# Spreads by transposes, a softmax without its sign flip, a new order of attention's weight loads, and eight fixed PSUM banks from the last head pair on

## The chip, the cores and the metric

The kernel runs on one core of one Trainium2 chip. The metric is the device time of one execution, in microseconds (us). A core has a matrix engine (TensorE, PE), a vector engine (VectorE, DVE), a scalar engine (ScalarE, ACT), GpSimd (POOL) and a queue that issues most DMAs (SyncE, SP). Each engine works through its own list of instructions in order and waits on semaphores for the others. TensorE writes to PSUM, eight banks of 512 float32 per partition.

## The reference, cut to what matters

One block of a network over 512 latent tokens of width 2048 and 256 context tokens, in float32:

```
mod = silu(c) @ w_ada + b_ada                       # six vectors of 2048, for shift, scale and gate
h   = modulate(rms_norm(x, g_mix), shift_a, scale_a)
qa, kva, kr, cb, cc, ch = split(h @ w_in)           # the context goes through the same weights
k, v = mla_key_value(kva, kr, g_kv, w_kv, rope)     # latent and context keys and values, 8 heads
q    = mla_query(qa, g_q, w_q, rope)                # rms_norm(qa, g_q) @ w_q
p    = softmax(q @ k.T * 192 ** -0.5)               # 512 queries, 768 keys
att  = p @ v
conv = cb * dwconv3(cc * ch)
x    = x + gate_a * (rms_norm per group of 128 of [att, conv]) @ w_out
hf   = modulate(rms_norm(x, g_ffn), shift_f, scale_f)
x    = x + gate_f * (a * silu(g)) @ w_down          # a, g = split(dwconv3(hf @ w_up))
out  = rms_norm(x, g_final)
```

## The kernel before, in words

Activations lie transposed, channels on partitions and tokens on columns. A product in float32 precision is made of three passes: each operand is split into a rounded high part (a CAST on ACT, names ending in `h`) and the rest (a subtraction on DVE, names ending in `l`), and TensorE adds high by high, low by high and high by low (`mm3`, L170 to L172). So every weight tile that arrives by DMA in a raw buffer costs an ACT and a DVE instruction before its matmuls.

The stages, in order of time: loads, norm and the first modulation vectors (to about 100 us); the input projection and the context (to 436); attention (to 652); the output projection, six of whose 16 output groups run as **rows** (`row`: one of 16 blocks of the input against six output groups, 18 matmuls, tiles `of`, to 714) and the other ten as **wholes** (`whole`, tiles `o6` to `o13`, then `o14` and `o15` by halves in the tile `ol`, to 831); the first three column groups of the up projection as rows again (tiles `uf`, to about 900); the other up products `u3`, `u4`, ... by a scheme of seven products for eight (tiles `u3a`, `u3b`, `u3c`; `u3p6`, `u3q5` are its weights), to 1683; the down projection to the end.

**Attention** is a loop of 32 steps, (head, quarter of the queries), in four pairs of heads. A step makes the scores two steps ahead (`scores`, tile `s`), takes a row maximum on DVE (L683), multiplies it by minus the scale (L684), does Exp on ACT with row sums (L687, tile `p`), transposes `p` on TensorE (L700, tile `t`), splits it (`pth`, `ptl`), and every second step multiplies with the values (`attend`, tile `po`). Spread through the loop are: the pieces of the next pair's queries, keys and values (`pieces`, weights `rq`, `rk`, loaded by `fetch`), the dots of the later modulation vectors (`late_dot`, L238: 1 MB `ra` loads by `late_load`, two DVE instructions of 1024 columns each), and the norms of finished heads: `merge_sum` makes the sums of a pair (tile `gs`), GpSimd takes a power (L732, tile `gr`), and `merge` spreads the result (tile `gb`). `late_bg` holds the same for the convolution's groups, four of them before the loop's steps and four behind them (`gn`, `acc21` to `acc30`). The `ra` loads and the weights of queries, keys and values share the two raw buffers of the pool `wp`.

A **spread** turns a column of 128 numbers into a 128 by 128 tile whose every row is that column: a matmul of the broadcast column with the identity (`spread`, L267, and the same in `merge`, L741).

A tile scheduler orders each engine's list from the program's order and its own estimates of durations; `keep` holds some instructions (the dots among them) in the program's order. PSUM is two pools' worth of rotating tiles: two tiles of two banks (`big`: `s`, `rs`, `ol`, parts of the rows) and four of one bank (`sml`: `t`, `po`, `gs`, `gb`, `pq`). When the up products from `u3` on begin, these pools are closed and eight fixed banks take their place (`bank_of`, `BANKS`).

When the rows of the up projection are through, `acts` does the width-3 convolution and the silu (L928 to L938, with one load of the Silu table) of their three column groups; its place is inside `u3`, between the products `p2` and `p6`.

## Time and profile before

| | |
|---|---|
| median of 3 runs | 2206.74 us (2206.45 to 2209.09) |
| the profiled execution | 2206.8 us, of which the span 2204.9 and 1.9 around it |
| PE busy in the span | 2149.2 us (97%) |
| DVE, ACT, POOL busy | 1599.0, 1010.5, 111.3 us |
| mean granted clock of TensorE | 0.996 |

Rows of the profile give a start or a stretch, the busy time, engine, line, operation and the tiles written and read; a bracket gives the idle time ahead of an instruction and the engine whose result ended it. A busy PE is a modelled figure: matmuls overlap, and a row that gives 0.28 us for one of 256 columns stands among rows that start every 0.12 us. The granted clock (PEclk) is 1.00 at full speed.

### The profile page before, as it was taken

What the parts mean: (1) busy time and instruction counts of PE and PEld (TensorE: products, weight loads), DVE (VectorE), ACT (ScalarE), POOL (GpSimd) and SP (SyncE); (2) the same over time, 40 slices, a digit from 0 to 9 for tenths busy, and PEclk for the clock granted to TensorE, in tenths of its full rate; (3) what the DMA queues carried; (4) which work ended last, traced back from release to release, by engine and by line L of the source; (5) the groups of instructions that cost most, each with busy time, mean ns of one, the idle gap of its engine ahead of it and who ended that gap; (6) DMA issues with size and microseconds to landing.
All of it is one profiled execution on the core that took longest, in us unless ns stands there. A gap on an engine that the chain in (4) does not pass through costs nothing.

```text
span 2204.9 us, 34542 instructions
## 1 busy us (share of the span) xinstructions
PE 2149.2 (97%) x13346; PEld 1914.2 (87%) x13346; DVE 1599.0 (73%) x2493; ACT 1010.5 (46%) x1635; POOL 111.3 (5%) x149
## 2 busy tenths in 40 slices
PE   7899999999999999999999999999999999999998
PEld 4688888878888888899999999999999888888887
DVE  7998887678896848777777777777777873633544
ACT  5523333544452237555554555555554432532444
POOL 0000000000000000011111011111110000000000
PEclk9999999999999999999999999999999999999999
DMA  8989884434469925577777777777776995753462
GB/s 331 344 276 334 275 279 150 144 120 149 158 235 358 331 86 172 132 196 201 204 194 195 201 205 195 194 201 201 201 193 200 350 345 159 247 164 92 160 210 88
DMA packets 144264, 466.75 MB, mean 212 GB/s; under 512 B 16290, under 2 KB 20642, under 8 KB 138082
## 3 DMA queue, kind: packets, MB, share of 16 engines
q1 hardware_dynamic: 125652, 405.03, 54.1%
q0 software_dynamic: 16272, 57.42, 12.8%
q8 instruction: 104, 1.70, 0.3%
q10 hardware_dynamic: 2176, 2.10, 0.3%
q14 instruction: 60, 0.49, 0.1%
HBM read 442.73 MB, written 20.71 MB: 210 GB/s over the span
## 4 chain that ended last, share of the span: by engine, by line
PE 91%; DVE 4%; DMA 2%; ACT 2%; issue 1%; SPq 0%; POOL 0%; DVEq 0%; ACTq 0%
PE d L170 7%; PE d L172 7%; PE d L171 7%; PE pp L170 4%; PE pp L172 4%; PE pp L171 4%; PE o L172 1%; PE o L171 1%; PE o L170 1%; PE uf L170 1%; PE uf L171 1%; PE uf L172 1%; PE of L172 1%; PE pf L171 1%; PE of L170 1%; PE of L171 1%
## 5 line engine op out<-in xcount | busy, mean ns | idle before, releaser
L997 POOL DMA_DIRECT2D u_s<-in_w_up x80 | 68.1, 851 | 416.3 <-DMA u_s<-in_w_up 353.4
L153 ACT CAST w_0h<-rw 128x512 fp32r<-128x512 f32 (+1 forms) x63 | 38.5, 618 | 107.3 <-PE pp L171 65.7
L216 DVE SCALAR_TENSOR_TENSOR ada<-ada,sv 128x1024 f32<-128x1024 f32 x64 | 77.4, 1217 | 4.6 <-DMA ada<-in_w_ada 4.6
L491 DVE SCALAR_TENSOR_TENSOR ada<-ada,svc 128x1024 f32<-128x1024 f32 x64 | 75.9, 1218 | 2.0 <-DMA ada<-in_w_ada 1.8
L238 DVE SCALAR_TENSOR_TENSOR ra<-ra,sv 128x1024 f32<-128x1024 f32 x50 | 59.4, 1216 | 0.0
L154 DVE TENSOR_TENSOR w_0l<-rw,w_0h 128x512 fp32r<-128x512 f32 (+1 forms) x63 | 42.4, 680 | 21.8 <-ACT w_0h L153 21.8
L238 DVE SCALAR_TENSOR_TENSOR ada<-ada,sv 128x1024 f32<-128x1024 f32 x46 | 55.7, 1218 | 2.6 <-DMA ada<-in_w_ada 2.6
L1108 DVE TENSOR_TENSOR u<-u,u 128x1024 f32<-128x1024 f32 x40 | 49.0, 1225 | 1.3
L1107 DVE TENSOR_TENSOR u<-u,u_s 128x1024 f32<-128x1024 f32 x40 | 48.7, 1217 | 0.0
L939 POOL DMA_DIRECT2D y_d<-a x43 | 24.7, 576 | 386.2 <-DVE a L938 376.7
L732 POOL TENSOR_TENSOR gr<-gr,half 128x8 f32<-128x8 f32 x4 | 8.3, 2084 | 641.4 <-DVE mx L684 505.3
L238 DVE SCALAR_TENSOR_TENSOR adl<-adl,sv 128x1024 f32<-128x1024 f32 x32 | 38.8, 1218 | 0.2 <-DMA adl<-in_w_ada 0.2
L683 DVE TENSOR_REDUCE mx<-s 128x1 f32<-128x768 f32 x32 | 30.4, 951 | 8.4 <-PE s L673 8.4
L704 DVE TENSOR_TENSOR ptl<-t,pth 128x384 fp32r<-128x384 f32 x64 | 33.2, 548 | 4.2 <-ACT pth L703 4.2
L502 DVE TENSOR_TENSOR acc<-acc,pp 128x512 f32<-128x512 f32 x50 | 33.9, 678 | 1.9 <-PE pp L172 1.8
L703 ACT CAST pth<-t 128x384 fp32r<-128x384 f32 x64 | 28.5, 488 | 14.3 <-PE t L700 14.1
L936 ACT ACTIVATE g<-g 128x512 f32<-128x512 f32 x43 | 27.2, 633 | 12.1 <-DVE g L930 12.1
L928 ACT ACTIVATE g<-cg,sm 128x512 f32<-128x512 f32 x40 | 32.5, 813 | 0.0
L687 ACT ACTIVATE p<-s,mx 128x768 f32<-128x768 f32 x32 | 29.3, 915 | 6.8 <-DVE mx L684 6.6
L928 ACT ACTIVATE a<-ca,sm 128x512 f32<-128x512 f32 x40 | 32.1, 802 | 0.0
L700 PE MATMUL t<-io,p 128*128 128x128 f32 x192 | 27.5, 274 | 3.7 <-ACT p L687 2.4
L929 DVE SCALAR_TENSOR_TENSOR g<-cg,sm,g 128x511 f32<-128x511 f32 x40 | 29.8, 745 | 0.0
(15580 smaller groups left out, 8734.8 us busy)
## 6 DMA issues: line engine op xcount, KB each, us to landing
ada<-in_w_ada SPq DMA_DIRECT2D x174, 512.0 KB, 6.0
u<-in_w_up SPq DMA_DIRECT2D x120, 512.0 KB, 8.3
u_s<-in_w_up SPq DMA_DIRECT2D x80, 512.0 KB, 4.1
u_s<-in_w_up POOLq DMA_DIRECT2D x80, 512.0 KB, 9.5
d<-in_w_dn SPq DMA_DIRECT2D x86, 384.0 KB, 3.8
y<-y_d SPq DMA_DIRECT2D x129, 256.0 KB, 4.5
ra<-in_w_ada SPq DMA_DIRECT2D x25, 1024.0 KB, 4.8
adl<-in_w_ada SPq DMA_DIRECT2D x32, 512.0 KB, 6.0
```

The lines of the kernel that those rows point to most:

```text
L153: A.copy(out=hi[:, :n], in_=raw[:, a:a + n])
L154: V.tensor_tensor(out=lo[:, :n], in0=raw[:, a:a + n], in1=hi[:, :n].bitcast(F32), op=ALU.subtract)
L170: PE.matmul(ps, w[0], x[0], start=first, stop=False, skip_group_check=on_top)
L171: PE.matmul(ps, w[0], x[1], start=False, stop=False, skip_group_check=on_top)
L172: PE.matmul(ps, w[1], x[0], start=False, stop=last, skip_group_check=on_top)
L216: V.scalar_tensor_tensor(out=r, in0=r, scalar=1.0, in1=vec[:, i * 1024:(i + 1) * 1024], op0=ALU.mult, op1=ALU.mult, accum_out=col[:, i:i + 1])
L238: keep(V.scalar_tensor_tensor(out=r, in0=r, scalar=1.0, in1=svs[i], op0=ALU.mult, op1=ALU.mult, accum_out=lc[:, t % 4:t % 4 + 1] if i else ...
L491: keep(V.scalar_tensor_tensor(out=raw[q], in0=raw[q], scalar=1.0, in1=svc[:, q * 1024:(q + 1) * 1024], op0=ALU.mult, op1=ALU.mult, accum_o ...
L928: A.activation(u, src, AF.Identity, bias=s("fb", m), scale=s("fw", 86 + m))
L997: G_.dma_start(r[-1], src[more], accum_op=ALU.add)
L1107: V.tensor_tensor(out=a11, in0=a11, in1=s1, op=ALU.add)
L1108: V.tensor_tensor(out=a12, in0=a12, in1=a11, op=ALU.add)
```

## The change

It has these parts:

1. The gain of the queries `g_q` is multiplied by minus the scale once at the start, so scores come out negative and scaled: a step takes the row minimum and Exp with scale -1, and the small multiplication L684 is gone (32 instructions).
2. `spread` is a transpose of the broadcast column against the identity, in place of a matmul, and `merge` uses it: 88 spreads in the whole kernel.
3. A dummy Exp stands behind the last square root ahead of attention, so that the Exp table is loaded there.
4. The loads of attention's weights are issued one to three steps ahead at the start of each pair, and the next pair's first piece `q_nope(1, 0)` stands ahead of the loop; the `ra` loads stand in six steps of eight, up to step 28 (22 of them, before 25); `merge` comes one step later, the last four convolution groups come in the steps 25, 27, 29 and 31, and the first two weights of the output projection's rows are loaded in the steps 29 and 30.
5. PSUM becomes eight fixed banks when the loop's steps end. The last `attend`, the last `merge_sum` and then four of the 16 rows (`OUT_EARLY`) come ahead of the last `merge`. `ol`, `uf` and the norm behind them get fixed banks, and the order of `BANKS` differs.
6. Of the three `acts` that stood inside `u3`, one stays there, one comes at the end of `u3`'s step and one at the end of `u4`'s.

```diff
-            PE.matmul(pb[:, g * P:(g + 1) * P], bc(r[:, g:g + 1], P), ident, start=True, stop=True)
+            PE.transpose(pb[:, g * P:(g + 1) * P], bc(r[:, g:g + 1], P), ident)
...
+        V.tensor_scalar(s("g_q", 0, 4), s("g_q", 0, 4), scalar1=-SCALE, scalar2=None, op0=ALU.mult)
...
-            mx = tiny(1, f"mx{hd}{tt}")
-            V.tensor_reduce(mx, ss[:, :768], axis=AX.X, op=ALU.max)
-            V.tensor_scalar(mx, mx, scalar1=-SCALE, scalar2=None, op0=ALU.mult)
+            mn = tiny(1, f"mn{hd}{tt}")
+            V.tensor_reduce(mn, ss[:, :768], axis=AX.X, op=ALU.min)
...
-            A.activation(pt, ss[:, :768], AF.Exp, bias=mx, scale=SCALE, accum_out=den[hd // 2][:, i:i + 1])
+            A.activation(pt, ss[:, :768], AF.Exp, bias=mn, scale=-1.0, accum_out=den[hd // 2][:, i:i + 1])
...
+        with tc.issue_after(roots[0]), tc.issue_after(roots[1]):
+            A.activation(tiny(1, "exp"), eps, AF.Exp)
+        fetch(1, 0)
+        late_load(ada_raw)
...
+        q_nope(1, 0)
+        fetch(1, 1)
...
-            elif n % 8 == 1 and n > 1:
+            if n % 8 == 2 and n > 8:
                 merge(n // 8 - 1)
             late_dot(1)
-            if n % 4 != 3:
+            if n > 24 and n % 2:
+                deque(late_bg[4 + (n - 25) // 2], 0)
+            at = n % 8
+            if at == 0 and n and n < 24:
+                fetch(pr + 1, 1)
+            if pr < 3 and n:
+                f, p_, i = pieces(pr + 1)[at]
+                f(p_, i)
+            if at < 2 and n < 24:
+                fetch(pr + 1, 2 + at)
+            elif at >= 2 and n < 29:
                 late_load(ada_raw)
-            if pr < 3:
-                f, p_, i = pieces(pr + 1)[n % 8]
-                f(p_, i)
-                if n + 1 < 24:
-                    fetch((n + 1) // 8 + 1, (n + 1) % 8)
+                if at == 6 and n < 16:
+                    fetch(pr + 2, 0)
+            if n in (29, 30):
+                k = 2 * (n - 29)
+                out_raw[k] = load(w_out_first[k // 2], 2 * G * P, f"ofr{k}")
...
+        ph_ps.close()
...
+        one_bank[0] = in_turn((6, 7))
         attend(7, 1)
         merge_sum(3)
-        for g in late_bg[4:]:
-            deque(g, 0)
+        pss = [bank_of(g, f"of{g}") for g in range(G)]
...
+        for k in range(OUT_EARLY):
+            if k % 2 == 0:
+                w = row_weights(w_out_first, k, "of", raw=out_raw[k])
+            out_row(k, w)
         merge(3)
...
-    pss = first_banks("uf")
+    pss = [bank_of(i, f"uf{g}") for g, i in enumerate((2, 3, 4, 5, 1, 0))]
...
-        while first_acts:
+        if first_acts and f == G // 2:
             acts(*first_acts.pop(0))
```

Three places show what the scheduler makes of it. The first is ACT at the first softmax; `p00` is the first Exp, `pth` the cast of a transposed tile, `wk1h`, `wv1h` and `wq11h` are casts of the next pair's weights, `q10h` that of its queries. Before:

```order
L300 CAST v02h_3888<-pv02_3875 128x512
L687 ACT_TABLE_LOAD
L687 ACTIVATE p00_3922,den0_3918<-s00_3896,mx00_3919 128x768
L687 ACTIVATE p01_3951,den0_3918<-s01_3907,mx01_3948 128x768
L703 CAST pth00_3953<-t000_3955 128x3x128
L703 CAST pth00_3953<-t001_3961 128x3x128
```

and now:

```order
L306 CAST v02h_3895<-pv02_3882 128x512
L155 CAST wv1h_4122<-rk1_4004 128x512
L306 CAST q10h_3943<-pq10_3930 128x512
L155 CAST wq11h_4178<-rq11_4066 128x512
L717 ACTIVATE p00_3924,den0_3921<-s00_3899,mn00_3922 128x768
L717 ACTIVATE p01_3975,den0_3921<-s01_3910,mn01_3973 128x768
L733 CAST pth00_3977<-t000_3979 128x3x128
```

The table load is gone from here, and three casts that wait for weights stand ahead of the first Exp.

The second is DVE at the end of attention; `ptl70` and `ptl71` feed the last two `attend`s (`po70`, `po71`), `ra54` and the like are late dots, `acc27` and `acc30` convolution groups, `mx0l` is the low part of the first row's input. Before:

```order
L704 TENSOR_TENSOR ptl70_5772<-t711_5829,pth70_5771 128x3x128
L238 SCALAR_TENSOR_TENSOR ra54_5816,mod_89<-ra54_5816,sv_92 128x1024
L238 SCALAR_TENSOR_TENSOR ra54_5816,lc_93<-ra54_5816,sv_92 128x1024
L704 TENSOR_TENSOR ptl71_5856<-t720_5857,pth71_5855 128x3x128
L704 TENSOR_TENSOR ptl71_5856<-t721_5863,pth71_5855 128x3x128
L729 TENSOR_TENSOR den6_5517<-den6_5517 128x8
L238 SCALAR_TENSOR_TENSOR ra55_5848,mod_89<-ra55_5848,sv_92 128x1024
L238 SCALAR_TENSOR_TENSOR ra55_5848,lc_93<-ra55_5848,sv_92 128x1024
L301 TENSOR_TENSOR mx0l_6012<-acc9_327,mx0h_6011 128x512
L704 TENSOR_TENSOR ptl71_5856<-t730_5896,pth71_5855 128x3x128
```

and now:

```order
L343 SCALAR_TENSOR_TENSOR acc27_672<-acc27_672,sm_81,gb6_5828 128x512
L734 TENSOR_TENSOR ptl70_5751<-t711_5809,pth70_5750 128x3x128
L734 TENSOR_TENSOR ptl71_5841<-t720_5842,pth71_5840 128x3x128
L246 TENSOR_TENSOR mod_89<-mod_89,sm_81 128x4
L240 SCALAR_TENSOR_TENSOR ra52_5744,lc_93<-ra52_5744,sv_92 128x1024
L759 TENSOR_TENSOR den6_5492<-den6_5492 128x8
L240 SCALAR_TENSOR_TENSOR ra53_5797,mod_89<-ra53_5797,sv_92 128x1024
L240 SCALAR_TENSOR_TENSOR ra53_5797,lc_93<-ra53_5797,sv_92 128x1024
L734 TENSOR_TENSOR ptl71_5841<-t721_5848,pth71_5840 128x3x128
L760 TENSOR_SCALAR den6_5492<-den6_5492 128x8
L307 TENSOR_TENSOR mx0l_5964<-acc9_328,mx0h_5963 128x512
L343 SCALAR_TENSOR_TENSOR acc30_709<-acc30_709,sm_81,gb7_5889 128x512
```

One dot less stands between `ptl70` and the third `ptl71`; a convolution group has come in.

The third is ACT inside `u3`, around `acts`: `g0`, `g1`, `g2` are the three groups' gates, `u3q5h` and `u3p7h` casts of the up products' weights. Before:

```order
L921 CAST u3p6h_8486<-u3_11_8195 128x1024
L928 ACTIVATE g2_8475<-uf4_7577,sm_81 128x512
L936 ACT_TABLE_LOAD
L936 ACTIVATE g0_8453<-g0_8453 128x512
L936 ACTIVATE g1_8464<-g1_8464 128x512
L936 ACTIVATE g2_8475<-g2_8475 128x512
L928 ACTIVATE a2_8480<-uf4_7577,sm_81 128x512
L921 CAST u3q5h_8516<-u3_s1_8199 128x1024
L1063 COPY u31_8420<-u3a_8387 128x256
L921 CAST u3p7h_8544<-u3_s3_8202 128x1024
```

and now:

```order
L972 CAST u3p6h_8446<-u3_11_8189 128x1024
L987 ACT_TABLE_LOAD
L987 ACTIVATE g0_8435<-g0_8435 128x512
L972 CAST u3q5h_8476<-u3_s1_8193 128x1024
L1100 COPY u31_8402<-u3a_8369 128x256
L972 CAST u3p7h_8504<-u3_s3_8196 128x1024
L987 ACTIVATE g1_8535<-g1_8535 128x512
```

One silu stands ahead of `u3q5h` in place of three.

More of the change, by code (lines that the diff above doesn't have):

```diff
@@ L34 @@
 EARLY = 6
-BANKS = [0, 1, 7, 4, 5, 6, 2, 3]
+BANKS = [7, 6, 2, 3, 4, 5, 1, 0]
+OUT_EARLY = 4
 CTX_EARLY = 6
@@ L573, in block_kernel, with half_of, row, row_weights @@
         del spare["w"]
+    HS = [slice(0, T // 2), slice(T // 2, T)]
+    def half_of(w, h):
+        return tuple(z[:, HS[h]] for z in w)
+    def row(pss, w, x, k, cols=slice(0, T)):
+        for g in range(G):
+            mm3(pss[g][:, cols], w[g], tuple(z[:, cols] for z in x), k == 0 and cols.start == 0, k == NK - 1)
+    def row_weights(src, k, nm, held=False, raw=None):
+        raw = load(src[k // 2], 2 * G * P, f"{nm}r{k}") if raw is None else raw
+        if held:
+            r = []
+            for b in range(0, 2 * G, 4):
+                w = hilo(raw[:, b * P:(b + 4) * P], 4 * P, f"{nm}w{k}_{b}")
+                r += [part(w, q) for q in range(4)]
+        else:
+            r = blocks(raw, 2 * G, f"{nm}w{k}")
+        return r[:G], r[G:]
     mixa = [None] * NH
@@ L739, in merge @@
                 pb_ = sml(f"gb{hd}")
-                for g in range(4):
-                    PE.matmul(pb_[:, g * P:(g + 1) * P], bc(r[:, i * 4 + g:i * 4 + g + 1], P), ident, start=True, stop=True)
+                spread(pb_, r[:, 4 * i:4 * i + 4])
                 o = oo[hd]
@@ L810, in ada_spare @@
         return ada_tiles(g_sb, 4, w_ada[t], f"ada{t}")
-    HS = [slice(0, T // 2), slice(T // 2, T)]
-    def half_of(w, h):
-        return tuple(z[:, HS[h]] for z in w)
-    def row(pss, w, x, k, cols=slice(0, T)):
-        for g in range(G):
-            mm3(pss[g][:, cols], w[g], tuple(z[:, cols] for z in x), k == 0 and cols.start == 0, k == NK - 1)
-    def row_weights(src, k, nm, held=False):
-        raw = load(src[k // 2], 2 * G * P, f"{nm}r{k}")
-        if held:
-            r = []
-            for b in range(0, 2 * G, 4):
-                w = hilo(raw[:, b * P:(b + 4) * P], 4 * P, f"{nm}w{k}_{b}")
-                r += [part(w, q) for q in range(4)]
-        else:
-            r = blocks(raw, 2 * G, f"{nm}w{k}")
-        return r[:G], r[G:]
     def whole(raw, xs, nm, ps=None, cols=slice(0, T), ld=None):
-        ps = bank(nm) if ps is None else ps
+        ps = sml(nm) if ps is None else ps
         per = 2048 // len(raw)
@@ L884, in x_tile @@
         SP.dma_start(xres[m], xt[:, m * T:(m + 1) * T])
[L886 to L887 removed]
+    for k in range(OUT_EARLY, NK):
         if k % 2 == 0:
             w = row_weights(w_out_first, k, "of")
[L890 to L892 removed]
+        out_row(k, w)
+        late_both(ada_spare if k % 4 < 3 or k == NK - 1 else None)
     for m in range(NK - 2):
```

47 lines of the change are left out of this document (24 added, 23 removed).

## The prediction

> **What bounds the kernel now.** I read the page's sums first, then the chain of waits, then busy time by stage, then TensorE's waits.
>
> ```profile
> PE 2149.2 (97%) x13346; PEld 1914.2 (87%) x13346; DVE 1599.0 (73%) x2493; ACT 1010.5 (46%) x1635; POOL 111.3 (5%) x149
> ...
> PE 91%; DVE 4%; DMA 2%; ACT 2%; issue 1%; SPq 0%; POOL 0%; DVEq 0%; ACTq 0%
> ```
>
> TensorE is busy for 97% and makes 91% of the chain. So the time falls by whatever matmul records disappear where PE is the bound, by idle time of PE that goes, and by nothing else. By stage (columns: length; busy time of PE, its weight loads, DVE, ACT, POOL; granted clock; DMA share; GB/s):
>
> ```profile
> 100.00:436.00 336.00, 334.23 (x1566) 274.81 (x1565) 284.47 (x546) 125.69 (x233) 0.00 (x0) 1.00 0.73 248
> ...
> 443.00:603.00 160.00, 150.50 (x988) 133.85 (x987) 129.19 (x252) 76.57 (x165) 4.15 (x2) 1.00 0.42 145
> 603.00:652.00 49.00, 44.03 (x309) 39.74 (x308) 46.30 (x91) 26.82 (x59) 4.19 (x2) 0.97 0.57 205
> 652.00:714.00 62.00, 62.00 (x270) 50.30 (x269) 45.05 (x78) 15.79 (x27) 1.28 (x2) 1.00 0.96 358
> ...
> 920.00:1683.00 763.00, 763.00 (x6430) 762.81 (x6429) 574.30 (x647) 400.17 (x535) 85.99 (x113) 1.00 0.74 197
> ```
>
> The projection, the rows and the up products are full: there only fewer or shorter matmuls help. Attention has room: 9.5 us of idle PE in its first 160 us, 5.0 in its last 49, where DVE is busy 46.30 of 49. The waits of PE (total, times, longest) name the rest:
>
> ```profile
> PE u3c L170 <- ACT u3q5h L921: 4.3, 1, 4.3
> ...
> PE s L669 <- ACT p L687: 3.4, 3, 1.5
> PE t L700 <- ACT p L687: 2.4, 2, 2.1
> PE po L171 <- DVE ptl L704: 2.4, 1, 2.4
> PE uf L170 <- ACT ufw0h L921: 1.7, 1, 1.7
> PE qr L342 <- ACT xq L591: 1.6, 2, 1.0
> PE pq L172 <- DVE wq12l L154: 1.3, 1, 1.3
> ...
> PE gb L741 <- POOL gr L732: 1.0, 1, 1.0
> ...
> PE pq L170 <- ACT wq11h L153: 0.9, 1, 0.9
> ```
>
> Some of these idles cost twice. Behind the waits of `po` and of `u3c` stand stretches in which the clock was granted at about half:
>
> ```profile
> 636.00:639.50 3.50, 3.50 (x18) 3.50 (x19) 3.50 (x9) 0.53 (x2) 0.00 (x0) 0.56 0.56 216
> ...
> 912.00:916.00 4.00, 3.87 (x19) 3.88 (x20) 3.97 (x5) 1.29 (x3) 0.54 (x1) 0.57 0.36 119
> ```
>
> 3.5 us at 0.56 lose 3.5 × 0.44 = 1.5 us, 4.0 at 0.57 lose 1.7. I count 1.7 for a window.
>
> **Spreads.** How a matmul and a transpose of float32 128x128 stand in the trace:
>
> ```profile
> L267 PE MATMUL gb<-io,gn x64: 270/275/421, 442.6 to 643.4; 128*128 128x128 f32 x64
> ...
> L741 PE MATMUL gb<-io,gr x64: 270/275/376, 510.6 to 652.0; 128*128 128x128 f32 x64
> L267 PE MATMUL rs<-io,rr x44: 270/275/581, 25.3 to 2195.4; 128*128 128x128 f32 x44
> ...
> L700 PE MATMUL t<-io,p 128*128 128x128 f32 x192 | 27.5, 274 | 3.7 <-ACT p L687 2.4 <-ACT o L716 0.9
> ...
> 614.32 1.95 PE L741 MATMUL gb<-io,gr 128*128 128x128 f32 x16
> 616.10 0.82 PE L700 MATMUL t<-io,p 128*128 128x128 f32 x6
> ```
>
> The program has 32 spreads of `gn` and 32 of `gr`, and each kind has 64 records: two each. It has 32 steps × 6 transposes, and these have 192 records: one each. 16 records last from 614.32 to 616.10, 0.111 us each; the six transposes behind them last 0.57, 0.095 each. So a spread costs 0.22 us and as a transpose about 0.11. 64 of them lie in attention: 7.1 us (3.55 ahead of 603, 3.55 behind). Of the other 24, ten of the latent and context norms stand in the full stage to 436 or at its edge, with two of the context's norm: 12 × 0.11 = 1.3 us; eight stand on the path in the two norms behind (four each, ffn and final): 0.4 each; four at the start, where DMAs and DVE decide, 0.3. From the one side this is sure (0.11 × 88 = 9.7 us, the most), from the other the least is nothing where DVE or a DMA decides, as in the last 49 us of attention.
>
> [...]
>
> **The first softmax.** The table load stood on the path:
>
> ```profile
> 447.33 1.28 ACT L687 ACT_TABLE_LOAD   x1 [3.90 <-DVE mx L684]
> 448.63 0.90 ACT L687 ACTIVATE p<-s,mx 128x768 f32<-128x768 f32 x1
> ...
> rq<-in_w_q SPq DMA_DIRECT2D x12, 256.0 KB, 2.7
> rk<-in_w_kv SPq DMA_DIRECT2D x4, 512.0 KB, 3.8
> ...
> L684 DVE TENSOR_SCALAR mx<-mx 128x1 f32<-128x1 f32 x26 | 3.8, 147 | 0.2
> ```
>
> 1.28 us go from there, to a place where DVE's reciprocal and the spread of the context's norm cover them. But `p00` now stands behind the cast `wq11h`. Its load follows `rk1` through one raw buffer: 3.8 us, two casts, then 2.7. By that chain `wq11h` ends near where the table load began, and `p00` starts about as late as now, while PE has `q_nope(1, 0)` (2.8 us) to do: of the wait of 2.1 us some 1.3 stays. The bounds: 0.6 to 2.
>
> [...]
>
> **The loop's steps to 603.** The small DVE instruction between the maximum and the Exp (147 ns as a row) leaves all 32 steps; a late dot leaves two steps of eight; weights come earlier. The waits of `s` (3.0 of the 3.4 lie here) and of `pq` (2.2) should go. `qr`'s wait stays: in the new order the cast `wq21h` stands ahead of `xq`, and I count 0.9 for each of two pairs. With 1.3 at the start and 1.5 of small ones, 4.6 us of idle remain. Now it is 9.5 by the row of the stage, and some 12 with the gaps inside busy stretches (starts of neighbouring matmuls against 0.23 us for 512 columns and 0.12 for 256). That is −7.4, and with the spreads −3.55: **−11**. Bounds: −7, where half of the waits only change their name, to −14.
>
> **The end of attention.** What DVE does from `o5` to the last `ptl71` (616.9 to 636.95) and what PE waits for:
>
> ```profile
> L238 DVE SCALAR_TENSOR_TENSOR ra<-ra,sv 128x1024 f32<-128x1024 f32 x9 | 10.7, 1216 | 0.0
> L704 DVE TENSOR_TENSOR ptl<-t,pth 128x384 fp32r<-128x384 f32 x12 | 6.3, 549 | 0.5 <-ACT pth L703 0.5
> ...
> L337 DVE SCALAR_TENSOR_TENSOR acc<-acc,sm,gb 128x512 f32<-128x512 f32 x8 | 5.8, 735 | 0.0
> ...
> 635.88 0.58 PE L171 MATMUL po<-ptl,v30h 128*128 128x256 f32 x1 [2.38 <-DVE ptl L704]
> ```
>
> DVE is the bound here. In the new order six dots stand in this stretch, not nine (−3.4 at 1.14 from start to start), one `mx` subtraction less (−0.6), two `ptl` less (−0.9), the idle of 0.5 goes, three `acc` come in (+2.0): 16.5 us instead of 20.0. PE has 13.6 us of work there with its spreads, so it still waits: some 1.7 us ahead of `po70` and 3 around `gb7` and `po71`. Against the same matmuls before this gives 3.8 us, or 2.1 if a half-clock window follows again. To it come the spreads (3.55), the wait for `gr` (1.0, covered by 72 matmuls of rows) and 0.5 of smaller ones. Against it stand the first row waiting for its weights behind three `mx` (0.6) and the third row for a cast behind ten `mx` and two dots (0.5). Together 6 to 7.8, I take **−7**; bounds −3 (two windows) to −11 (DVE keeps up).
>
> **The rows and wholes** to 809 are full, keep their matmuls, and stay: 0. **`uf`**: the cast `ufw0h` comes behind one more ACT copy, and sums stand ahead of the first matmul: +0.4 (0 to +1), the window behind it stays.
>
> **`u3`.** PE waits for the cast `u3q5h`, which stands behind all three silus, each of which waits for DVE:
>
> ```profile
> 912.13 0.58 PE L170 MATMUL u3c<-T10h,u3q5h 128*128 128x256 f32 x1 [4.32 <-ACT u3q5h L921]
> ...
> 904.92 0.63 ACT L936 ACTIVATE g<-g 128x512 f32<-128x512 f32 x1
> 907.92 0.63 ACT L936 ACTIVATE g<-g 128x512 f32<-128x512 f32 x1 [2.37 <-DVE g L930]
> 909.84 0.63 ACT L936 ACTIVATE g<-g 128x512 f32<-128x512 f32 x1 [1.29 <-DVE g L930]
> 911.04 1.03 ACT L921 CAST u3q5h<-u_s 128x1024 fp32r<-128x1024 f32 x1
> ```
>
> Now one silu stands ahead, and no `g2`: the cast starts near 904.8 and ends at 905.8, when PE is still in `u3b` (to 907.6). `u3c` lies in the bank of `uf0`, whose last reader on DVE ends about 903.4. The third `acts` goes into `u4`, where DVE is idle a quarter of the time (574.30 busy of 763) and the four instructions that read `uf4` and `uf5` fit ahead of `u5p1`. So 4.5 us go and the window with them: **−6.2**; at least −4, if `u3p7` or `u5p1` waits instead.
>
> **Sum**, against the profiled 2206.8 (span 2204.9 and 1.9 around it; the median of the runs, 2206.74, is the same): −0.3 − 1.3 − 11 − 7 + 0.4 − 0.4 − 6.2 − 0.4 = −26.2, so **2180.6**.
>
> **The rivals.**
>
> - *The waits of attention change place* (chance 0.17). ACT and DVE work in order, and casts of weights stand ahead of Exps at three pair starts. For it: `wq11h` ahead of `p00`. Against: DVE is busy 129 of 160, so it catches up. Then the steps bring 5, the end 3: −15.2, 2191.6.
> - *Attention loses nearly all its idle time* (0.15): −14 and −11, with the rest as above: −33.2, 2173.6.
> - *A transpose with a broadcast operand takes two records* (0.05), so that the spreads bring nothing: −26.2 + 9.4 = −16.8, 2190.0. For it: no transpose of the trace has such an operand.
> - *Transposes don't keep the clock up* (0.08). Runs of them, with a short idle, would bring half-clock windows, 1.7 us each: at the end of attention, where `gb7` stands between two waits, and in the two norms behind: two or three more, 2185. Against: 192 transposes stand in a stretch at 1.00. [...]
> - *Slower* (0.03): weights of a pair and the 1 MB `ra` loads go through two raw buffers, each held until DVE's dots are through. If each of the 24 pieces of pairs 1 to 3 is late by more than 1.1 us, the 26 us are eaten; at 2 us each it is 48 − 26 = 22 slower, 2228. Against: pieces cost 2.7 us in all now, and fewer `ra` loads compete.
>
> The forecast itself has 0.52, own range 2176 to 2187.
>
> **The numbers.** Low: the second rival with 1.6 us more, 2172. High: the first rival, 2192. What lies outside is the slower case and the far ends of these two, some 0.15. A measurement here can tell 0.2%, 4.4 us. Faster by more, so under 2202.3: all cases but the last, 0.97, less 0.02 for the first rival's far end: 0.95; within: 0.02; slower: 0.03.
>
> **What would show it.** Right: 88 records fewer with `io` and one record to each spread; no ACT_TABLE_LOAD between the first scores and `p00`; no wait of `u3c` and clock 1.00 at 912 less the gain; the wait for `gr` gone, and the largest waits of attention at `po70` and `po71`. Wrong: `s` or `t` waiting in each pair's first steps for `p` behind a `wq` cast; `of` waiting for `ofw`; a new wait at `u5a`.

## The result, and the profile after

The changed kernel takes 2186.89 us (median of 4 runs, 2178.99 to 2188.47) where the kernel before takes 2207.91 beside it (4 runs, 2206.45 to 2211.14): a ratio of 0.9896, 95% interval 0.9868 to 0.9923. On another chip it is 0.9876 (0.9849 to 0.9902). The profiled execution is one of 2188.47 us, span 2186.6, against the 2206.8 and 2204.9 of before: 18.3 us less, where 26.2 were predicted.

First the sums of the page and of its chain of waits, after the change:

```profile
PE 2144.9 (98%) x13258; PEld 1913.1 (87%) x13258; DVE 1594.5 (73%) x2462; ACT 1010.9 (46%) x1636; POOL 112.9 (5%) x149
...
PE 94%; DVE 3%; DMA 2%; ACT 1%; issue 0%; SPq 0%; DVEq 0%; ACTq 0%
```

The matmul records fall by 88, from 13346 to 13258, but PE's busy time only by 4.3 us. The stages of the changed kernel (columns as before: length; busy time and count of PE, its weight loads, DVE, ACT, POOL; granted clock; DMA share; GB/s) say where. The stretches are shifted by what came earlier; the last row is the up stage, which stood at 920 to 1683 before:

```profile
443.00:603.00 160.00, 158.09 (x1057) 142.61 (x1057) 136.77 (x243) 82.06 (x176) 7.54 (x3) 1.00 0.44 149
603.00:640.00 37.00, 32.61 (x188) 28.79 (x187) 34.53 (x65) 21.27 (x44) 1.92 (x1) 0.86 0.59 205
...
898.00:1664.00 766.00, 766.00 (x6385) 766.00 (x6384) 573.72 (x649) 399.37 (x535) 86.42 (x114) 1.00 0.74 197
```

In the first 160 us of attention PE is idle for 1.9 us where it was 9.5. At its end the clock falls to 0.86 in the mean. And the up stage, which is full in both kernels, now needs 766 us for 6385 matmuls where it started 6430 in 763: 120.0 ns for each, not 118.7.

I cut the span at the first matmul of a few tiles (the starts are from the timeline of PE, in the profiled executions; the third column is a second profiled execution of the changed kernel, on another chip):

| from ... to the first matmul of the next | before, us | after | again | predicted |
|---|---|---|---|---|
| start, projection, to the first scores | 436.2 | +0.2 | -1.1 | -1.6 |
| attention and the rows, to the last `of` | 277.9 | -16.0 | -17.7 | -18 |
| wholes, to the last `o13` | 89.5 | -0.3 | -0.3 | 0 |
| `ol` and the norm, to `uf` | 28.1 | -1.6 | -1.5 | +0.4 - 0.4 |
| `uf` | 70.1 | -2.2 | -2.2 | 0 |
| `u3` | 17.6 | -6.0 | -6.0 | -6.2 |
| `u4` to `u42` | 757.6 | +8.5 | +8.5 | 0 |
| down, final norm | 527.9 | -0.9 | -2.3 | -0.4 |
| span | 2204.9 | -18.3 | -22.5 | -26.2 |

A second profiled execution of the kernel before (it stands among the experiments) takes 439.7 us in the first row, 280.8 in the second, 68.7 in `uf` and 525.7 in the last, so in these rows differences of up to 3 us are no more than the scatter of executions; in the `u3` row it takes 17.3, and in the `u4` to `u42` row 757.6 again. So the terms for attention and `u3` are near their sizes, `ol` and the norm bring more than was counted, and one stage that "stays" grows by 8.5 us. The waits of PE in the changed kernel (total, times, longest) show no `u3c`, no `gb` for `gr`, no `pq` for weights:

```profile
PE rs L289 <- DVE fq0t L324: 1.7, 1, 1.7
PE po L172 <- DVE den L760: 1.5, 1, 1.5
PE po L173 <- DVE ptl L734: 1.4, 1, 1.4
...
PE s L699 <- ACT p L717: 1.1, 2, 0.7
PE t L730 <- DVE ptl L734: 1.0, 1, 1.0
...
PE uf L172 <- ACT ufw0h L972: 0.3, 1, 0.3
```

The first row is new: PE waits for the sums of the norm right ahead of `uf`. The two largest waits of attention are at `po`, as predicted, but both at the last value product, `po71`; `po70` waits 0.2 us, behind the 1.0 of `t` (615.20 below). The timeline of PE there, and then the same stretch by windows, with its clock:

```profile
615.20 0.55 PE L730 MATMUL t<-io,p 128*128 128x128 f32 x3 [0.99 <-DVE ptl L734]
...
620.93 0.35 PE L172 MATMUL po<-pth,v30h 128*128 128x256 f32 x1 [1.48 <-DVE den L760]
622.64 0.58 PE L173 MATMUL po<-ptl,v30h 128*128 128x256 f32 x1 [1.35 <-DVE ptl L734]
```

```profile
621.50:632.00 10.50, 9.36 (x35) 8.49 (x36) 10.50 (x19) 8.93 (x18) 0.00 (x0) 0.51 0.62 215
```

Three waits of 1.0 to 1.5 us lie within 8 us. The clock falls at 621.8, within the last of them, and stays at half for 10.2 us (10.5 in the row, with its edges), in which matmuls of 256 columns start every 0.21 us. That costs some 5 us. The window behind `uf` and the one in `u3` are gone; but the one behind `uf` is missing in the second profiled execution of the kernel before, too.

A second stretch at half clock, 6.8 us long, lies in the start of this execution; the second profiled execution of the change doesn't have it. Both, in this order:

```profile
55.00:63.00 8.00, 7.03 (x20) 5.04 (x19) 8.00 (x17) 3.56 (x7) 0.00 (x0) 0.57 0.94 346
```

```profile
55.00:63.00 8.00, 5.74 (x25) 4.03 (x23) 8.00 (x17) 4.44 (x10) 0.00 (x0) 1.00 0.98 385
```

In the profiled executions of the changed kernel and its variants below, the first scores come at 436.4 to 438.3 us where this stretch stands (six executions) and at 434.0 to 436.4 where it doesn't (five).

Each spread has one record now, where it had two (forms of PE's instructions on the tile `gb`, then on `rs`):

```profile
L273 PE MATMUL gb<-io,gn x32: 270/272/294, 446.6 to 619.2; 128*128 128x128 f32 x32
...
L273 PE MATMUL gb<-io,gr x32: 270/272/273, 512.0 to 648.3; 128*128 128x128 f32 x32
...
L273 PE MATMUL rs<-io,rr x22: 270/272/475, 25.3 to 2176.5; 128*128 128x128 f32 x22
```

The table load stands ahead of attention, and the first Exp right behind the cast `wq11h`, which waits for its weights (ACT in the changed kernel):

```profile
435.38 1.28 ACT L794 ACT_TABLE_LOAD   x1
...
447.62 0.62 ACT L155 CAST wq11h<-rq 128x512 fp32r<-128x512 f32 x1 [1.46 <-DMA rq<-in_w_q]
448.14 0.90 ACT L717 ACTIVATE p<-s,mn 128x768 f32<-128x768 f32 x1
```

In `u3` the cast that was waited for comes right behind the first silu:

```profile
883.58 1.28 ACT L987 ACT_TABLE_LOAD   x1 [0.56 <-DVE g L981]
884.88 0.63 ACT L987 ACTIVATE g<-g 128x512 f32<-128x512 f32 x1
885.41 1.04 ACT L972 CAST u3q5h<-u_s 128x1024 fp32r<-128x1024 f32 x1
```

### The profile page after: what moved, and what is told of

Its sections match the earlier page's. It is cut to its first block, busy times and chain, and to the rows that moved or that the text cites. A ratio compares the mean times of both kernels' runs of the same rounds, so it can differ in the third digit from the quotient of the medians.

```text
span 2186.6 us, 34349 instructions
## 1 busy us (share of the span) xinstructions
PE 2144.9 (98%) x13258; PEld 1913.1 (87%) x13258; DVE 1594.5 (73%) x2462; ACT 1010.9 (46%) x1636; POOL 112.9 (5%) x149
## 4 chain that ended last, share of the span: by engine, by line
PE 94%; DVE 3%; DMA 2%; ACT 1%; issue 0%; SPq 0%; DVEq 0%; ACTq 0%
PE d L172 7%; PE d L173 7%; PE d L174 7%; PE pp L172 4%; PE pp L174 4%; PE pp L173 4%; PE o L172 1%; PE o L173 1%; PE o L174 1%; PE of L172 1%; PE of L173 1%; PE of L174 1%; PE uf L172 1%; PE uf L174 1%; PE uf L173 1%; PE pf L173 1%
## 5 line engine op out<-in xcount | busy, mean ns | idle before, releaser
L218 DVE SCALAR_TENSOR_TENSOR ada<-ada,sv 128x1024 f32<-128x1024 f32 x64 | 78.0, 1226 | 4.3 <-DMA ada<-in_w_ada 4.0
L240 DVE SCALAR_TENSOR_TENSOR ada<-ada,sv 128x1024 f32<-128x1024 f32 x52 | 62.7, 1222 | 7.1 <-DMA ada<-in_w_ada 7.1
L156 DVE TENSOR_TENSOR w_0l<-rw,w_0h 128x512 fp32r<-128x512 f32 (+1 forms) x63 | 43.0, 688 | 22.5 <-ACT w_0h L155 20.4
L240 DVE SCALAR_TENSOR_TENSOR ra<-ra,sv 128x1024 f32<-128x1024 f32 x44 | 52.6, 1222 | 1.1 <-DMA ra<-in_w_ada 1.0
L714 DVE TENSOR_REDUCE mn<-s 128x1 f32<-128x768 f32 x32 | 30.5, 955 | 4.8 <-PE s L703 4.6
L717 ACT ACTIVATE p<-s,mn 128x768 f32<-128x768 f32 x32 | 29.3, 916 | 1.6 <-DVE mn L714 1.3
L980 DVE SCALAR_TENSOR_TENSOR a<-ca,sm,a 128x511 f32<-128x511 f32 x40 | 29.8, 746 | 0.0
```

The source lines that it names most:

```text
L156: V.tensor_tensor(out=lo[:, :n], in0=raw[:, a:a + n], in1=hi[:, :n].bitcast(F32), op=ALU.subtract)
L218: V.scalar_tensor_tensor(out=r, in0=r, scalar=1.0, in1=vec[:, i * 1024:(i + 1) * 1024], op0=ALU.mult, op1=ALU.mult, accum_out=col[:, i:i + 1])
L240: keep(V.scalar_tensor_tensor(out=r, in0=r, scalar=1.0, in1=svs[i], op0=ALU.mult, op1=ALU.mult, accum_out=lc[:, t % 4:t % 4 + 1] if i else ...
```

## The experiments

Two things were to be explained: what the single terms are worth, and why the up stage, whose instructions on PE are the same in both kernels but for banks and addresses, has become slower by 8 us. Line numbers are those of the changed kernel; `-` is what stands in it, unless the text says otherwise.

**The two kernels again.** No edit.

> The kernel before, unchanged, for a trace on the same chip as the changed one. In the profiled pair the matmuls of the up products follow each other every 118.7 ns before and every 119.9 after, 7.1 us over the stage, though none of them was changed. If the chip or the execution makes it, this run shows about 119.9 too; if the change makes it (by banks or by where the tiles lie), it shows 118.7. Either theory: three half-clock windows of 3.4 us, time 2206 to 2211.

> The change, unchanged, to see how its time is spread. Theory: its times differ (2179 to 2188 so far) by the half-clock stretch at the end of attention, 10.2 us long in the profiled execution, none in the one of 2179 us; so the times of this run go down as the mean granted clock goes up, 1 us for each 0.0005, and span times clock stays within 2 us of 2174. Rival: the times differ for another reason, and span times clock spreads over 9 us like the times themselves.

Before took 2209.15 us in its one run, the change 2184.85 (6 runs, 2179.62 to 2190.2); before's own runs beside them were 2206.34 to 2220.52. The numbers of matmuls in the same 700 us of the up stage repeat on this other chip. In order: before and the change as first profiled, then both again:

```profile
940.00:1640.00 700.00, 700.00 (x5902) 700.00 (x5901) 530.69 (x598) 368.01 (x491) 80.01 (x106) 1.00 0.74 199
```

```profile
940.00:1640.00 700.00, 700.00 (x5835) 700.00 (x5834) 523.73 (x592) 365.33 (x488) 78.92 (x104) 1.00 0.74 197
```

```profile
940.00:1640.00 700.00, 700.00 (x5901) 700.00 (x5901) 530.76 (x599) 369.35 (x494) 79.51 (x105) 1.00 0.74 199
```

```profile
940.00:1640.00 700.00, 700.00 (x5835) 700.00 (x5835) 524.76 (x592) 364.65 (x487) 79.49 (x105) 1.00 0.74 197
```

700 us over 5902 is 118.6 ns, over 5835 it is 120.0, at clock 1.00 and with PE never idle. So this is no chance of one execution. The change's own runs differ by up to 10 us, and this goes with the clock: the profiled one of 2184.15 has 0.997, those of 2190.2 and 2179.62 have 0.994 and 0.998. Span times mean clock, which is roughly the time at full clock, is 2173 to 2177 for all six. The profiled execution of before has five stretches at half clock ahead of the down projection, of 3.4 or 6.8 us, where three were expected.

**Spreads as matmuls**, all else as in the change:

```
-            PE.transpose(pb[:, g * P:(g + 1) * P], bc(r[:, g:g + 1], P), ident)
+            PE.matmul(pb[:, g * P:(g + 1) * P], bc(r[:, g:g + 1], P), ident, start=True, stop=True)
```

> The change with spreads as matmuls again, everything else as in the change. Prediction: 88 records of 0.11 us come back, 9.7 us, of which 7 to 9 reach the time where the engine is the bound: span times clock near 2182. Rival 1: DVE decides attention's end and the spreads there cost nothing: 4 to 5 us. Rival 2 (transposes don't keep the clock up): the half-clock stretch at the end of attention is gone or shorter with matmuls, and the time is about that of the change, 2184 to 2188, with a clock of 0.996 or more.

2191.5 us (2188.08 to 2194.86; ratio to before 0.9904, 0.9877 to 0.9932), 6.7 more than the change on the same chip; span times clock is 2182.0 in the mean against 2175.2, 6.8 more. So the transposes bring about 6.7 us and not 9.5. Attention with its rows is 3.3 us longer here than in the first profiled execution of the change, which has as much half clock there; 7.1 were counted. At its end DVE sets the pace (busy for 18.00 us of the 18 from 618 on), and longer spreads fill PE's waits: from the first scores to 652 these are 6.8 us in the change and 3.5 in this kernel, 3.1 of them in three rows,

```profile
PE po L172 <- DVE ptl L734: 1.5, 1, 1.5
PE gb L273 <- DVE ptl L734: 1.2, 1, 1.2
PE t L730 <- DVE ptl L734: 0.3, 1, 0.3
```

and the half-clock stretch is there with matmuls as well (the windows of this kernel):

```profile
618.00:636.00 18.00, 15.12 (x75) 13.39 (x74) 18.00 (x34) 13.40 (x28) 0.00 (x0) 0.72 0.64 212
```

So it needs no spreads by transposes; the transposes of `t`, which stand in every kernel here, are not tested. The stretch is 10.2 us long here too, as in the first profiled execution of the change. One execution says little of its length, which differs between executions of one kernel: in the second one of the change it is 6.8 us (clock 0.69 from 619 to 630). This kernel also has the window at the start of `uf` back (that stage is 2.2 us longer than in the change). Its up stage has 120.0 ns too.

**All three `acts` at their old place**:

```
-        if first_acts and f == G // 2:
+        while first_acts:
             acts(*first_acts.pop(0))
```

> The change with all three acts inside the first up step again, nothing else. Prediction: 4.5 us of waiting for the cast of u3q5 come back and with them a window of half clock, 6.2 us in all, so 6 us slower than the change. Rival: the fixed banks made the gain, not the place of acts; then within 2 us of the change.

2187.43 us (2186.69 to 2189.86; ratio 0.9888, 0.9861 to 0.9915): as the change. `u3` is still 6.0 us shorter than before, and nothing waits for `u3q5h`: its cast stands behind one silu here as well (ACT in this kernel).

```profile
884.85 0.63 ACT L987 ACTIVATE g<-g 128x512 f32<-128x512 f32 x1
885.39 1.04 ACT L972 CAST u3q5h<-u_s 128x1024 fp32r<-128x1024 f32 x1
...
888.74 0.62 ACT L987 ACTIVATE g<-g 128x512 f32<-128x512 f32 x1
```

So the 6 us do not come from the place of `acts`, on which the prediction put them. What is left are the other parts, with which the scheduler finds this order by itself; the fixed banks are the likeliest, but they were not taken out alone.

**The old order of banks in the changed kernel, and the new one in the kernel before.**

```
-BANKS = [7, 6, 2, 3, 4, 5, 1, 0]
+BANKS = [0, 1, 7, 4, 5, 6, 2, 3]
...
-        one_bank[0] = in_turn([6 * h])
+        one_bank[0] = in_turn([h])
...
-    pss = [bank_of(i, f"uf{g}") for g, i in enumerate((2, 3, 4, 5, 1, 0))]
+    pss = [bank_of(i, f"uf{g}") for g, i in enumerate((7, 4, 5, 6, 2, 3))]
```

In the kernel before only the first of these lines is changed, the other way round.

> The change with the eight banks taken in the order of before (0, 1, 7, 4, 5, 6, 2, 3) by the up and down products, and the rows of the up projection and the norm's bank shifted so that the first steps are as free as in the change; every tile of the up products lies at the same address as in the change. The kernel before on this chip has 118.9 ns from one up matmul to the next, all changed ones 120.0. If the order of the banks makes it: 118.7 here, the up stage 7 to 8 us shorter, time near 2177. If the addresses of the tiles make it (35 of 56 operands lie elsewhere than before): 120.0 and the time of the change, 2185.

> The kernel before with the changed order of the banks and nothing else; every operand of the up products lies where it lay before. If the order of the banks makes the difference: 120.0 ns between up matmuls, the stage 7 to 8 us longer, time near 2217. If the addresses make it: 118.7 to 118.9, time near 2209.

The first takes 2187.22 us (6 runs, 2180.79 to 2188.39; ratio 0.9882, 0.9856 to 0.9908), the second 2209.22 in one run. The up stages don't change with the banks; the change with old banks, then before with new ones:

```profile
940.00:1640.00 700.00, 700.00 (x5836) 700.00 (x5835) 525.99 (x592) 365.30 (x488) 78.63 (x104) 1.00 0.74 196
```

```profile
940.00:1640.00 700.00, 700.00 (x5901) 700.00 (x5900) 530.82 (x599) 369.07 (x493) 79.49 (x105) 1.00 0.74 199
```

The order of the banks is not the cause. Nor is it what freed `u3`: the first keeps the 6.0 us. But in the kernel before it moves the waits in `u3`. The new order leaves no wait for `u3q5h`, and three shorter ones at the first matmuls of `u3a`, `u3b` and `u3c` (waits of PE from 820 to 960):

```profile
PE u3b L170 <- ACT g L936: 2.0, 1, 2.0
...
PE u3a L170 <- DVE g L930: 1.5, 1, 1.5
PE u3c L170 <- DVE a L930: 1.1, 1, 1.1
```

Its matmuls start every 118.7 ns from the first of `u3a` on. So the rhythm goes with the waits in these runs: with either order of the banks it is the fast one where PE waits in `u3`, and the slow one where it doesn't. In the profiled execution of the change with old banks attention ends without any half-clock stretch, though the waits are those of the change,

```profile
618.00:636.00 18.00, 15.17 (x82) 12.94 (x82) 18.00 (x32) 12.71 (x25) 0.00 (x0) 1.00 0.74 258
```

and its stage "attention and the rows" is 20.4 us shorter than before, not 16.0. Its time, 2180.79, is that of the change's fastest runs.

**What the waits at the end of attention cost: late dots at other steps.** First the last three at the steps 24 to 26 instead of 26 to 28; then the last two of them taken out of the loop and put into the rows behind it:

```
-            elif at >= 2 and n < 29:
+            elif (at >= 2 or n >= 24) and n < 27:
```

```
-            elif at >= 2 and n < 29:
+            elif at >= 2 and n < 27:
...
-        late_both(ada_spare if k % 4 < 3 or k == NK - 1 else None)
+        late_both(ada_spare)
```

> The change with the last three late loads issued in steps 24 to 26 in place of 26 to 28, so that the late dots end two steps earlier; nothing else. Theory (DVE, by the dots among the splits, makes the waits ahead of the last two value products, and these start the half-clock stretch): waits of po and of the last t fall from 3.8 to under 2 us, the half-clock stretch is gone in most executions, 3 to 7 us faster than the change. Rival (the stretch comes from something else, such as runs of transposes): waits fall by 2, the clock stays.

> The change with two late loads fewer in attention (20, the steps 27 and 28 load nothing) and the two in rows of the output projection that had none. Four dots (4.6 us of DVE) leave the stretch ahead of the last value products; the low parts of the first rows' weights (2.4 us) come into it. Theory (DVE's load there makes the waits, the waits the half-clock stretch): waits of po and t at the end fall from 3.8 to about 1 us, the clock is 0.997 or more in most executions, 3 to 6 us faster than the change. Rival (the stretch depends on where the clock's windows lie, not on 2 us of waiting): the same clocks as the change, 1 to 2 us faster. The rows can pay it back: they are at 0.96 of the DMA, and 2 MB more are 5.6 us of it.

The first is 2187.76 us (2186.64 to 2188.72; ratio 0.9889, 0.9853 to 0.9925). It did not do what it was made for: the scheduler put other work of DVE where the dots had been, and PE waits as much, at other places (its largest waits in attention):

```profile
PE po L172 <- DVE ptl L734: 2.3, 1, 2.3
PE t L730 <- DVE acc L343: 1.9, 1, 1.9
```

So it says nothing on the theory. The second is 2184.83 (2180.19 to 2187.12; ratio 0.9855, 0.9827 to 0.9884, beside a median of 2217.49 for before there). Its profiled execution has no half-clock stretch at the end of attention, though the waits of `po` and `t` there fall only from 4.0 to 2.9 us, not to 1 as expected. But its runs spread as the change's do, and at full clock it takes 2174.8 where the change takes 2175.2: no gain can be told.

**The table load back in front of the first Exp** (the dummy Exp taken out):

```
-        with tc.issue_after(roots[0]), tc.issue_after(roots[1]):
-            A.activation(tiny(1, "exp"), eps, AF.Exp)
```

> The change without the dummy Exp, so the table is loaded in front of the first softmax again, behind the cast wq11h. Prediction: 1.3 us longer wait of the first transposes. Rival: the load runs while that cast waits for its weight, or the first transposes wait for something else, and nothing moves.

One run, 2183.74 us. The wait for the first `p` grows by 1.4 us, from 1.1 to 2.5 in the sum of its kind, and the load stands on the path again (waits in attention; ACT):

```profile
PE s L699 <- ACT p L717: 2.5, 2, 2.1
```

```profile
445.26 0.62 ACT L155 CAST wq11h<-rq 128x512 fp32r<-128x512 f32 x1 [1.46 <-DMA rq<-in_w_q]
445.90 1.28 ACT L717 ACT_TABLE_LOAD   x1
447.19 0.90 ACT L717 ACTIVATE p<-s,mn 128x768 f32<-128x768 f32 x1
```

That is the 1.28 us of the load and little more. One execution's time can't tell 1.4 us; the wait can.

**Interruptions in the up stage.** In the first traces one more difference stood beside the two spacings. In the kernel before, matmuls start every 120 ns in `u3` too, up to the wait of 4.3 us for `u3q5h`, and every 118.7 once the 3.4 us of half clock behind this wait are over. In the change this wait is gone, and the 120 stay. The theory: there are two rhythms that hold themselves, and an interruption picks one. To test it, small matmuls of one column were put into the stream of the changed kernel, some of which wait for a copy on ACT (or for a chain of three copies) of the product just made, so that PE pauses:

```
+    KICKS = {6: 0, 10: 1, 14: 2, 18: 0, 22: 1, 26: 2, 30: 0, 34: 1, 38: 2}
+    def kick(f, pb):
+        t = bank_of(BANKS[(3 * (f - G // 2) + 3) % 8], f"kick{f}")
+        src = ones[:, 0:1]
+        if KICKS[f]:
+            src = tiny(1, f"ks{f}")
+            A.copy(out=src, in_=pb[:, 255:256])
+        if KICKS[f] > 1:
+            V.tensor_copy(src, src)
+            A.copy(out=src, in_=src)
+        return PE.matmul(t[:, 0:1], ident, src, start=True, stop=True).ins
```

> The change with nine extra matmuls of one column in the up stage, whose results nobody reads: three that wait for nothing (steps 6, 18, 30), three that wait for a copy of the product just made (10, 22, 34; about 1 us of idle TensorE) and three that wait for three copies in a row (14, 26, 38; about 2 us). What they are for: the matmuls of this stage come every 120.0 ns in all changed kernels, in a pattern of three, and every 118.7 in before, in a pattern of five. Neither the order of the banks nor the addresses of the tiles made the difference. Theory: both patterns hold themselves, and an interruption of TensorE picks one (before: the wait ahead of u3's second product); so behind some of these kicks the spacing is 118.7 to 118.9 until the next. Rival: something lasting in the changed program makes 120.0; then it is 120.0 behind all nine, and the time is that of the change plus some 9 us.

One run, 2201.61 us, with all its pauses. Stretches between and behind the small matmuls, and the first pause in the timeline of PE:

```profile
940.00:1020.00 80.00, 80.00 (x669) 80.00 (x669) 59.89 (x68) 41.97 (x56) 9.12 (x12) 1.00 0.74 198
1030.00:1100.00 70.00, 70.00 (x592) 70.00 (x591) 54.30 (x63) 37.68 (x50) 7.41 (x10) 1.00 0.74 200
...
1275.00:1345.00 70.00, 70.00 (x592) 70.00 (x592) 54.92 (x63) 38.12 (x51) 7.39 (x10) 1.00 0.74 201
1362.00:1402.00 40.00, 40.00 (x335) 40.00 (x335) 29.93 (x35) 21.02 (x28) 4.55 (x6) 1.00 0.66 169
1410.00:1510.00 100.00, 100.00 (x845) 100.00 (x844) 75.56 (x86) 52.50 (x70) 11.32 (x15) 1.00 0.74 198
...
1352.00:1362.00 10.00, 10.00 (x73) 10.00 (x74) 3.39 (x4) 3.81 (x5) 0.85 (x1) 0.85 0.92 203
1600.00:1640.00 40.00, 40.00 (x323) 40.00 (x323) 28.24 (x32) 19.93 (x27) 2.97 (x5) 0.95 0.67 171
```

```profile
1024.59 0.38 PE L1141 MATMUL kick<-ks,io 128*128 128x1 f32 x2 [1.08 <-ACT ks L1137]
```

A small matmul without a wait (at 914) leaves the rhythm as it was: 669 in 80 us, as many as in the change, where before has 677. The first pause, of 1.1 us at 1024.6, flips it: 592 in 70 us, the fast rhythm (the change has 585), and this holds for 320 us through pauses of 2.6 and 1.1 us. The pause of 2.6 us at 1351 is followed by a half-clock stretch (clock 0.85 from 1352 to 1362), and behind that stands the slow rhythm, 335 in 40 us (the change has 336), one matmul every 120.0 ns. The small matmul at 1405, without a wait, brings the fast one back: 845 in 100 us (the change has 836). The last pause, of 2.6 us at 1597.6, has 6.8 us of half clock behind it, and the fast rhythm holds, 118.7 ns behind 1604: half clock alone doesn't bring the slow one. So both rhythms occur in one execution, with the same instructions, banks and addresses before and behind; what differs is how the stream was interrupted last.

**One pause, early in the stage**, and the same together with the dots of above:

```
-    KICKS = {6: 0, 10: 1, 14: 2, 18: 0, 22: 1, 26: 2, 30: 0, 34: 1, 38: 2}
+    KICKS = {6: 1}
```

Here `-` is the line of the experiment before; the second kernel has the two edits of the late dots as well.

> The change with one extra matmul of one column in up step 6, which waits for a copy of the product just made, and nothing else: TensorE is idle for about 1.2 us once. Theory: it puts the up stage from the pattern of three (120.0 ns) into that of five (118.7), 36 steps of 168 matmuls at 1.33 ns are 8.0 us, less 1.4 for the pause: 6 to 7 us faster than the change, near 2178, span times clock near 2168. Rival: the pattern falls back, or the pause at step 10 did it by where it stood; then 1.4 us slower than the change.

> The same pause, and two late loads moved from attention to the rows. Theory: 0 to 3 us better than with the pause alone (fewer half-clock windows at the end of attention), 2175 to 2178. Rival: the loads only move DVE's work, and it equals the run with the pause alone.

One pause gives 2178.34 us (5 runs, 2176.29 to 2179.47), a ratio of 0.9848 to before (0.9822 to 0.9874): the fastest version of this study, and its slowest run is at the change's fastest. The change itself was not run on this chip. Its pause and what follows (timeline of PE, windows):

```profile
939.27 0.38 PE L1141 MATMUL kick<-ks,io 128*128 128x1 f32 x2 [1.07 <-ACT ks L1137]
939.51 0.37 PE L172 MATMUL u5a<-T40h,u5q4h 128*128 128x256 f32 x1
```

```profile
940.00:1640.00 700.00, 700.00 (x5901) 700.00 (x5901) 528.99 (x596) 367.43 (x490) 80.36 (x106) 1.00 0.74 198
```

66 matmuls more than in the change start in these 700 us, 7.8 us of time, for a pause that costs 1.6 by the starts of its neighbours: `u4` to `u42` takes 759.7 us in both kernels of this experiment, 766.1 in the change. At full clock the runs with one pause take 2168.6 in the mean, 5 to 7 less than the change's. With the dots it is 2178.4 (2178.15 to 2181.3; ratio 0.9852, 0.9826 to 0.9878): no more than the pause alone.

## Why the prediction was right and wrong

The forecast was 2180.6 us with a range of 2172 to 2192; the median is 2186.89. The direction and the range were right. That the sum came 6 us short has one cause that the sum did not have, and some terms that were off in both directions.

- **"The rows and wholes ... 0" and the up stage, called full at 920 to 1683.** This is the step that failed. A stage in which PE is busy without a gap, with the same instructions, was taken to keep its time. It took 8.5 us more, since its matmuls start every 120.0 ns in place of 118.7. By what the runs show, the wait of 4.3 us in `u3`, which was worth removing by itself, had also set the rhythm of the 6400 matmuls behind it. Shown are the two rhythms, that they are not the order of the banks, and that one pause of 1.1 us switches to the fast one. That the wait in `u3` did so in the kernel before is read from its traces: the spacing changes behind the wait, and with the new banks, where shorter waits stand earlier, it is the fast one earlier. The wait was not put back alone.
- **The spreads, 9.5 us of the sum.** One record each, as said: the rival of two records falls. But the size is 6.7. The working gave 3.55 to each half of attention, and named the condition, "nothing where DVE or a DMA decides, as in the last 49 us", without using it.
- **The loop's steps, -11 and the end, -7.** Together -16.0 and -17.7 in the two profiled executions, against -18. The idle time of the first 160 us fell from 9.5 to 1.9, 7.6 where 7.4 were counted with the smaller gaps. PE waits for no weights of pieces there any more, and the rival in which the waits change place falls: `s` and `t` wait 1.1 and 1.0 in all.
- **"a half-clock window again".** The bound for the end of attention held two windows, which lose 1.7 us each; the profiled execution has 10.2 us at half clock, which lose some 5. The same waits stand in executions with 0, 3.4 and 6.8 us of it. The 20.4 us of the execution without it, against 18, suggest that the gain of the work itself was put too small by some 2 us, about the scatter of that row, and that the clock took back 0 to 5 us of it. The rival "Transposes don't keep the clock up" has nothing for it: with the spreads as matmuls the stretch stays, at 10.2 us. Of the 192 transposes that the working sets against it, 48 stand behind 603, where the row has 0.97 and not 1.00.
- **`u3`, -6.2.** It is -6.0, and "Now one silu stands ahead" holds. But the working led it back to the place of `acts`, the third of which "goes into `u4`", and this failed: with all three at the old place one silu stands ahead too, and the gain stays. Which of the other parts frees the scheduler is open; the order of `BANKS` is not it.
- **`uf`, +0.4, "the window behind it stays".** The +0.4 is about right: PE waits 1.7 us for the sums and 0.3 for the cast ahead of `uf`, 2.0 in all, where the cast alone was waited for 1.7. What the sum lacks are the two waits of `ol` for its weights, 0.7 us each, which are gone; they make up most of the -1.6 there. The window is luck: behind `uf` it stands in one of two profiled executions of the kernel before, in neither of the change, and in some of its variants (the spreads as matmuls, the table load at its old place, nine small matmuls, one pause with the late dots). Without it `uf` takes 68.7 us before and 67.9 after, so 0.8 of the 2.2 are the change's at most.
- **The first softmax: 0.6 to 2.** The load is worth 1.4 us, as the run without the dummy Exp shows, and 1.28 of it is the load's own row. The first scores come hardly earlier (+0.2 and -1.1 against -1.6): the start varies by more than that term, with the half-clock stretch at 55 us among its reasons.
- **The slower rival** (raw buffers) has nothing for it: PE waits for no weights in attention.
- **A slip in the rivals.** With 5 for the steps and 3 for the end the terms of the first rival add up to -16.2, so 2190.6, and not to -15.2; the upper bound of 2192 came from it and was 1 us too high. The six transposes beside the spreads start every 0.109 us, not 0.095, which changes no term.

What stays open: why an interruption picks one rhythm or the other (in the kernel with nine small matmuls, of three interruptions that met the slow rhythm, two switched it, and of the six that met the fast one, one did; half clock stood behind that one, but also behind one that switched nothing); and what decides whether the same three waits are followed by no half clock or by 10 us of it.

## What to carry to other kernels

A stage in which the bounding engine never idles can still change its time when nothing in it changes: count the matmuls in a fixed stretch before and after, since busy shares and waits don't show it (PE is busy for 700.00 of 700 us at 5902 matmuls and at 5835). When a stall is removed, look at what followed it, not only at its length; here a stall of 4.3 us went and brought 6 us, the stage behind it then took 8.5 us more, and a pause of 1.1 us put into it won 6 of these back. Where an engine off the path sets the end of a stage, shorter work on the path there goes in part into its waits: of the 7.1 us counted for the spreads in attention, 3.3 came.

## What the runs showed of the hardware that was not expected

- **Two rhythms of matmuls.** Float32 products of 128x256 by rounded operands start every 118.7 or every 120.0 ns at clock 1.00, in patterns of five (115, 117, 122, 120, 119) and of three (118, 120, 122, or 117, 120, 123), and hold either through the 700 us that were counted (5902 matmuls before, 5835 in the change). Matmuls of 512 columns, in the output projection and in `uf`, start every 232.4 ns in both kernels. From `u4` to `u42` the two rhythms differ by 8.5 us (757.6 against 766.1). The kernel before has single runs of 2217 to 2222 us at mean clocks of 0.991 to 0.994, where its runs of 2204 to 2212 have 0.992 to 0.996; the slow rhythm would make such a difference, but no such run was traced.
- **Half clock after short waits.** Waits of 1.0, 1.5 and 1.35 us within 8 us went with 0, 3.4, 6.8 or 10.2 us at half clock in profiled executions of kernels with the same waits; these lengths are none, one, two and three times 3.4 us. The starts of the half-clock stretches of one execution lie whole multiples of 3.41 us apart, too: 58 and 23 of them in the first profiled execution of before (635.7, 833.6 and 912.1), 166 in that of the change (55.2 and 621.8). What decides how long the half clock lasts after the same waits was not shown. Span times clock is 2173 to 2177 us for all runs of the change, so most of their spread of 2179 to 2190 goes with the clock: with the stretch at the end of attention, and with the one of 0 or 6.8 us at 55 us. How the two share it in the runs without a trace is not known.
